# A modulation matrix loaded by channel chunks: the opening of a conformer and dilated-attention block on one Trainium2 core

## The chip, the cores and the metric

The kernel runs on one core of a Trainium2 chip. The metric is the device time of one execution in microseconds (us), as the median of several runs. Five engines run at once, each through its own instructions in a fixed order: TensorE (PE; its weight loads are listed as PEld), VectorE (DVE), ScalarE (ACT), GpSimd (POOL), and SyncE (SP), which here issues nearly all DMAs. An engine whose next instruction waits for a semaphore holds up everything behind it.

## The reference

One layer of a decoder block over 2048 tokens of 1024 channels, in float32. A conditioning vector `c` gives a shift and a scale per channel, the tokens are normalized and modulated, and one wide projection feeds a convolution branch and twelve attention heads:

```python
mod = silu(c) @ w_ada + b_ada                      # (1024) x (1024, 3072)
shift, scale, gate = jnp.split(mod, 3, axis=-1)
h = rms_norm(x, norm_w) * (1.0 + scale) + shift    # (2048, 1024)
z = h @ w_in                                       # a, b, g_conv, q, k, v, g_attn, m_conv, m_attn
q = rope(rms_norm(q, q_norm_w), positions); k = rope(rms_norm(k, k_norm_w), positions)
o = softmax-weighted sum of three dilated window attentions (4 heads each)
y = sigmoid(m_conv) * (conv branch @ w_conv_out) + sigmoid(m_attn) * (o * silu(g_attn) @ w_attn_out)
x = x + gate * (y @ w_out)
```

## The kernel before

Tokens go in 16 blocks of 128, channels in 8 chunks of 128. The modulated tokens `h` are kept transposed in SBUF for the whole projection, as two float32r parts `hT_hi` and `hT_lo`; each weight is split in the same way into `wh` and `wl`, and a projection is three matmuls per chunk (hi by wh, hi by wl, lo by wh), 24 for a block of tokens and 384 columns (`pz`, L305).

The program starts in this order. `c`, the biases and norm weights come in (`nat`, turned to `cols`); `sc` is silu of `c`. The rotary tables `tab` for all 16 blocks are made by DVE in operations over 1024 columns (L138 to L155), with two Sin on ACT. `w_ada`'s first 2048 columns come in 16 DMAs of whole rows (`wada`, L161), and PE multiplies `sc` with them in 64 matmuls (L163); the result is copied, turned into columns by 16 transposes (L171) and made into `mod` (L172, L173), which holds shift and scale for all channels. Only then can `h_first` make the first two token blocks of `h` (L223 to L230).

Then come the *units*: a unit is one attention head, with its 384 weight columns (q, k, v). Unit 0 has the extra work of making `h`: for a pair of token blocks, `x` is loaded (L190), squared and scaled on ACT (L199, L207) with the inverse root on POOL (L202, L106, L107), turned by PE (`pt_x`, L217, in four pieces of two chunks), and `h_part` makes `hf` (DVE, L238), `hT_hi` (ACT, L241) and `hT_lo` (DVE, L242). The piece for pair j+2 is turned inside the matmuls of blocks j and j+1. After its 24 matmuls each block has an end (`project_step`): squares on ACT (L322), inverse root on POOL, then on DVE norm weights (`qk`, L333), rotation (L340 to L343), and a store to `qkv_d` (L656). `t` banks of PSUM, two of them, take the turned pieces.

PE's order is that of the code, by hand. The other engines' orders are set by a list scheduler when the kernel is built, with its own estimates of durations; only instructions marked `keep_in_program_order` keep their place. A tile pool with `bufs=n` gives n buffers to a tag; a load into a buffer waits until all readers of the tile before it are done.

Of the kernel before, what the change touches and what calls it, by code (L numbers as in the profile page):

```python
# [10 lines left out]
F32 = mybir.dt.float32  # L11
# [7 lines left out]
P = 128  # L19
# [35 lines left out]
def tile_hybrid_block(  # L55
# [55 lines left out]

    tab = tabs.tile([P, NB, 2, 64], F32, tag="tab", name="tab0")
    with pool("start", side="right") as st:
        nat = st.tile([4 * KC, P], F32, name="nat")
        cols = st.tile([P, 4 * KC], F32, name="cols")
        nc.sync.dma_start(nat[:KC, :], c.rearrange("b (k p) -> (b k) p", p=P))
        nc.sync.dma_start(nat[KC : 3 * KC, :], b_ada[: 2 * D].rearrange("(k p) -> k p", p=P))
        nc.sync.dma_start(nat[3 * KC :, :], norm_w.rearrange("(k p) -> k p", p=P))
        nc.sync.dma_start(wqk[:, 0, :], q_norm_w[None, :].to_broadcast([P, P]))
        nc.sync.dma_start(wqk[:, 1, :], k_norm_w[None, :].to_broadcast([P, P]))  # L120
        pos_i = st.tile([P, NB], I32, name="pos_i")
        nc.sync.dma_start(pos_i, positions.rearrange("b (j p) -> p (b j)", p=P))
        freq = st.tile([P, 64], F32, name="freq")
        nc.sync.dma_start(freq, inv_freq[None, :].to_broadcast([P, 64]))

        pt = bank("t", "pt_c")
        nc.tensor.transpose(pt[:, : 4 * KC], nat, ident[: 4 * KC, : 4 * KC])
        nc.vector.tensor_copy(cols, pt[:, : 4 * KC])
        th = st.tile([P, KC], F32, name="th_c")
        nc.scalar.activation(th, cols[:, :KC], AF.Tanh, scale=0.5)  # L130
        nc.vector.scalar_tensor_tensor(sc, th, 1.0, cols[:, :KC], op0=ALU.add, op1=ALU.mult)
        nc.vector.tensor_scalar(sc, sc, 0.5, None, op0=ALU.mult)

        pos_f = st.tile([P, NB], F32, name="pos_f")
        nc.vector.tensor_copy(pos_f, pos_i)
        a = tab[:, :, 0, :]
        n = tab[:, :, 1, :]
        nc.vector.tensor_tensor(a, pos_f[:, :, None].to_broadcast([P, NB, 64]),  # L138
                                freq[:, None, :].to_broadcast([P, NB, 64]), op=ALU.mult)

        na = st.tile([P, NB, 64], F32, name="na")
        nc.vector.tensor_scalar(n, a, 1.0 / (2 * math.pi), MAGIC, op0=ALU.mult, op1=ALU.add)
        nc.vector.tensor_scalar(n, n, -MAGIC, None, op0=ALU.add)
        nc.vector.tensor_scalar(na, n, MAGIC * 2048, None, op0=ALU.add)
        nc.vector.tensor_scalar(na, na, -MAGIC * 2048, None, op0=ALU.add)
        nc.vector.tensor_sub(n, n, na)
        for part in TWO_PI:
            for t in (na, n):
                nc.vector.scalar_tensor_tensor(a, t, -part, a, op0=ALU.mult, op1=ALU.add)
        nc.vector.tensor_scalar(a, a, -PI_LO, PI_LO, op0=ALU.max, op1=ALU.min)  # L150
        nc.scalar.activation(n, a, AF.Sin)
        nc.scalar.activation(a, a, AF.Sin, scale=0.5)
        tc.keep_in_program_order(nc.scalar.activation(th[:, :1], th[:, :1], AF.Exp))
        nc.vector.tensor_tensor(a, a, a, op=ALU.mult)
        nc.vector.tensor_scalar(a, a, -2.0, 1.0, op0=ALU.mult, op1=ALU.add)  # L155

        acc = [bank("z", "ada0"), bank("z", "ada1"), bank("s", "ada2"), bank("s", "ada3")]
        for k in range(KC):
            for half in range(2):
                wa = st.tile([P, D], F32, tag="wa", name=f"wada{k}_{half}", bufs=10)  # L160
                last_ada = nc.sync.dma_start(wa, w_ada[P * k : P * k + P, D * half : D * half + D])  # L161
                for i in range(2):
                    nc.tensor.matmul(acc[2 * half + i][:1, :], sc[:, k : k + 1], wa[:, 512 * i : 512 * i + 512],  # L163
                                     start=(k == 0), stop=(k == KC - 1))
        row = st.tile([1, 2 * D], F32, name="row")

        for i in range(4):
            nc.scalar.activation(row[:, 512 * i : 512 * i + 512], acc[i][:1, :], AF.Copy)
        pa = bank("z", "pt_ada")
        for k in range(2 * KC):  # L170
            nc.tensor.transpose(pa[:, k : k + 1], row[:, P * k : P * k + P], ident[:1, :1])  # L171
        nc.vector.tensor_add(mod, pa[:, : 2 * KC], cols[:, KC : 3 * KC])  # L172
        nc.vector.scalar_tensor_tensor(mod[:, KC:], mod[:, KC:], 1.0, cols[:, 3 * KC :], op0=ALU.add, op1=ALU.mult)  # L173

# [12 lines left out]
    def load_x(j):  # L187

        xt = xp.tile([P, D], F32, tag="x", name=f"x{j}")
        i0 = nc.sync.dma_start(xt, x2[P * j : P * j + P, :])  # L190
        if j >= 4:
            tc.keep_in_program_order(i0)
# [27 lines left out]
    def h_first(kk, pt):  # L220
        for a in range(2):
            k = 2 * kk + a
            nc.scalar.activation(hi[:, k, :256], pt[:, 256 * a : 256 * a + 256], AF.Identity,  # L223
                                 scale=mod[:, KC + k : KC + k + 1], bias=mod[:, k : k + 1])
        for a in range(2):
            k = 2 * kk + a
            hf = xp.tile([P, 2, 256], F32, tag="hf", name=f"hf0_{k}", bufs=2)
            nc.vector.tensor_scalar(hf[:, 0], pt[:, 256 * a : 256 * a + 256], mod[:, KC + k : KC + k + 1],
                                    mod[:, k : k + 1], op0=ALU.mult, op1=ALU.add)
            (nc.gpsimd if a else nc.vector).tensor_tensor(lo[:, k, :256], hf[:, 0], hi[:, k, :256].bitcast(F32),  # L230
                                                          op=ALU.subtract)

# [11 lines left out]
    with tc.high_priority():  # L244
        for j in range(4):
            for f in load_x(j):
                f()
        turned = [h_turn(0, kk, "ttoo"[kk]) for kk in range(4)]

# [10 lines left out]
    def load_w(src, parts, tag, odd=None, pin=False, eng=nc.vector):  # L260
# [3 lines left out]
        def load(k):  # L264
            raw = wp.tile([P, 384], F32, tag="raw", name=f"raw_{tag}_{k}", bufs=3)
            off = 0
            for first, count, step in parts:
                w = P * count
                dst = raw[:, off : off + w].rearrange("p (s c) -> p s c", c=P)
                rowsk = src[P * k : P * k + P, :]  # L270
                if count == 1:
                    nc.sync.dma_start(raw[:, off : off + w], rowsk[:, first : first + P])
                else:
                    blk = rowsk.rearrange("p (s c) -> p s c", c=P)
                    b0, bs = first // P, step // P
                    nc.sync.dma_start(dst, blk[:, b0 : b0 + bs * (count - 1) + 1 : bs, :])
                off += w
# [20 lines left out]
    def z_tokens(pz, width, wh, wl, j, hooks, lo_last=False):  # L298
        terms = [(k, a, w[k]) for k in range(KC) for a, w in ((hi, wh), (hi, wl), (lo, wh))]
        if lo_last:  # L300
            terms.sort(key=lambda t: t[1] is lo)
# [220 lines left out]
    with tc.high_priority():  # L522
        for f in loads:
            f()
# [592 lines left out]
```

## Time and profile before

| | |
|---|---|
| median of 3 runs | 2532.13 us (2531.29 to 2532.79) |
| the profiled execution | 2532.06 us, of which the span is 2530.3 us |
| PE busy, of the span | 2495.4 us (99%) |
| DVE busy | 1663.2 us (66%) |
| ACT busy | 756.8 us (30%) |
| DMA, mean | 110 GB/s |

All times in the views are us from the span's start. A row of the timeline gives start, duration, engine, line, operation, output and inputs, shapes, how many, and in brackets how long the engine had been idle and for what it waited. "PEclk" is the granted clock of TensorE as a share of full speed.

### The profile page before, as it was taken

The page shows a single profiled execution, that of the slowest core. Times are in us where ns is not written, and L with a number is a line of the kernel's source. Part 1 is how long each engine was busy: PE and PEld are TensorE (multiplying, and loading weights), DVE is VectorE, ACT ScalarE, POOL GpSimd, SP SyncE. Part 2 cuts the span into 40 slices and gives each one's busy share as a digit, 9 for nine tenths or more (in the row PEclk, how much of TensorE's full clock was granted, in tenths as well). Part 3 has the DMA queues.
Part 4 walks back from the last instruction along what each step waited for, and adds up shares of the span by engine and source line. Part 5 has one row for each costly group of instructions (what it writes and reads, how often), then busy time and mean ns, then how long its engine had stood idle before and what let it go on. Part 6 is the DMA issues. An engine that isn't in the chain of part 4 may idle for free.

```text
span 2530.3 us, 38239 instructions
## 1 busy us (share of the span) xinstructions
PE 2495.4 (99%) x13377; PEld 2222.5 (88%) x13377; DVE 1663.2 (66%) x3522; ACT 756.8 (30%) x2366; POOL 250.1 (10%) x503
## 2 busy tenths in 40 slices
PE   7999999999999999999999999999999999999999
PEld 3989999999999999999888888888888878888887
DVE  5855655555555555566799999879697718774333
ACT  5733343344334434444111111111111114331010
POOL 3421111111111111122000000000000000000000
PEclk9999999999999999999999999999999999999999
DMA  6333533344321111144112122121212249867343
GB/s 228 116 106 113 160 111 97 100 118 122 108 75 55 56 36 40 52 130 149 41 47 70 64 80 83 39 70 60 63 65 68 99 147 328 296 211 230 124 134 111
DMA packets 262653, 278.51 MB, mean 110 GB/s; under 512 B 25464, under 2 KB 195736, under 8 KB 262462
## 3 DMA queue, kind: packets, MB, share of 16 engines
q1 hardware_dynamic: 262462, 276.07, 34.3%
q8 instruction: 106, 1.74, 0.3%
q14 instruction: 85, 0.70, 0.1%
HBM read 175.12 MB, written 100.86 MB: 109 GB/s over the span
## 4 chain that ended last, share of the span: by engine, by line
PE 95%; DMA 2%; ACT 1%; DVE 1%; POOL 1%; issue 0%; SPq 0%; POOLq 0%; DVEq 0%; ACTq 0%
PE pz L305 30%; PE pg L755 20%; PE yc L897 7%; PE out L897 7%; PE pb L755 7%; PE pa L755 7%; PE ya L897 3%; PE pzg L305 3%; PE ps L377 3%; PE po L396 3%; PE ptq L367 2%; PE ptp L388 1%; PE ada L163 1%; DMA fraw<-in_w_attn_out_dram 1%; DMA raw_u<-in_w_in_dram 0%
## 5 line engine op out<-in xcount | busy, mean ns | idle before, releaser
L784 DVE SCALAR_TENSOR_TENSOR ca<-up,chan,ca 128x1024 f32<-128x1024 f32 x480 | 593.2, 1280 | 3.7
L305 PE MATMUL pz<-wh_u,hT_lo 128*128 128x384 f32 x1536 | 536.2, 349 | 1.3 <-POOL hT_lo L230 0.7
L305 PE MATMUL pz<-wh_u,hT_hi 128*128 128x384 f32 x1536 | 516.9, 337 | 5.3 <-ACT wh_u L281 2.6
L305 PE MATMUL pz<-wl_u,hT_hi 128*128 128x384 f32 x1536 | 517.7, 337 | 0.6 <-DVE wl_u L284 0.4
L333 DVE SCALAR_TENSOR_TENSOR qk<-pz,st,wqk 128x128 f32<-128x128 f32 x384 | 116.9, 346 | 332.2 <-POOL st L107 332.1
L755 PE MATMUL pg<-hT_hi,wh_gm 128*128 128x512 f32 x768 | 298.7, 389 | 0.3 <-DVE gt L815 0.3
L755 PE MATMUL pg<-hT_lo,wh_gm 128*128 128x512 f32 x768 | 298.6, 389 | 0.0
L755 PE MATMUL pg<-hT_hi,wl_gm 128*128 128x512 f32 x768 | 297.9, 389 | 0.0
L305 PEld LDWEIGHTS pz<-wh_u,hT_hi 128*128 128x128 f32 x1536 | 289.7, 189 | 8.7 <-ACT wh_u L281 3.5
L305 PEld LDWEIGHTS pz<-wh_u,hT_lo 128*128 128x128 f32 x1536 | 289.2, 188 | 3.5 <-POOL hT_lo L230 1.3
L305 PEld LDWEIGHTS pz<-wl_u,hT_hi 128*128 128x128 f32 x1536 | 288.8, 188 | 1.8 <-DVE wl_u L284 1.4
L369 ACT ACTIVATE qkT<-ptq 128x256 f32<-128x256 f32 x192 | 74.0, 385 | 419.2 <-PE ptq L367 418.6
L813 ACT ACTIVATE gt<-pg 128x512 f32<-128x512 f32 x96 | 57.1, 597 | 422.2 <-PE pg L755 422.2
L755 PEld LDWEIGHTS pg<-hT_hi,wh_gm 128*128 128x128 f32 x768 | 144.1, 188 | 30.7 <-DVE gt L815 0.7
L755 PEld LDWEIGHTS pg<-hT_hi,wl_gm 128*128 128x128 f32 x768 | 144.2, 188 | 30.0
L755 PEld LDWEIGHTS pg<-hT_lo,wh_gm 128*128 128x128 f32 x768 | 144.1, 188 | 29.7
L107 POOL TENSOR_TENSOR st<-st,mhalf 128x2 f32<-128x2 f32 x192 | 136.7, 712 | 16.0
L322 ACT ACTIVATE sq<-pz 128x128 bf16<-128x128 f32 x384 | 106.2, 277 | 93.2 <-PE pz L305 86.4
L106 POOL TENSOR_SCALAR st<-st 128x2 f32<-128x2 f32 x192 | 45.7, 238 | 811.8 <-ACT sq L322 811.8
L382 ACT ACTIVATE sm<-sm,osb 128x128 f32<-128x128 f32 (+1 forms) x192 | 88.8, 462 | 64.4 <-DVE osb L380 61.3
L755 PE MATMUL pb<-hT_hi,wh_ab 128*128 128x512 f32 x256 | 99.7, 389 | 0.0
L755 PE MATMUL pa<-hT_hi,wh_ab 128*128 128x512 f32 x256 | 99.6, 389 | 0.0
(332 smaller groups left out, 4639.0 us busy)
## 6 DMA issues: line engine op xcount, KB each, us to landing
qkv_d<-qkv SPq DMA_DIRECT2D x128, 192.0 KB, 2.2
raw_u<-in_w_in_dram SPq DMA_DIRECT2D x96, 192.0 KB, 3.1
lqk<-qkv_d SPq DMA_DIRECT2D x128, 128.0 KB, 2.2
acc_d<-osb SPq DMA_DIRECT2D x192, 65.0 KB, 1.6
at<-acc_d SPq DMA_DIRECT2D x64, 195.0 KB, 3.3
x<-in_x_dram SPq DMA_DIRECT2D x16, 512.0 KB
wada<-in_w_ada_dram SPq DMA_DIRECT2D x16, 512.0 KB, 7.1
lv<-qkv_d SPq DMA_DIRECT2D x128, 64.0 KB, 1.8
```

The costliest lines, as they stand in the source:

```text
L107: nc.gpsimd.tensor_tensor(dst, scratch[:, :n], mhalf[:, :n], op=ALU.pow)
L305: nc.tensor.matmul(pz[:, :width], a[:, k, P * j : P * j + P], w[:, :width], start=(m == 0), stop=(m == 23))
L322: nc.scalar.activation(sq, pz[:, P * i : P * i + P], AF.Square, scale=1.0 / math.sqrt(P), accum_out=st[:, i : i + 1])
L333: nc.vector.scalar_tensor_tensor(qk[:, 2 * i : 2 * i + 2].rearrange("p a b -> p (a b)"), pz[:, P * i : P * i + P], st[:, 2 + i : 3 + i], w ...
L369: nc.scalar.activation(qkT.rearrange("p a b -> p (a b)"), pt[:, :256], AF.Copy)
L377: nc.tensor.matmul(ps[:, P * i : P * i + P], box["q"][:, 0, :], kt[:, 1, :], start=True, stop=True)
L382: nc.scalar.activation(sm[:, :w], sm[:, :w], AF.Exp, scale=-1.0, bias=o[:, P : P + 1], accum_out=o[:, P + 1 : P + 2])
L396: nc.tensor.matmul(po[:, :P], box["pT"][:, P * i : P * i + P], vt, start=(i == 0), stop=(i == nk - 1))
L755: nc.tensor.matmul(pz, w[k][:, P * col : P * col + P], a[:, k, 512 * t : 512 * t + 512], start=(m == 0), stop=(m == 23))
L784: nc.vector.scalar_tensor_tensor(accs[c], up[:, t0 + i : t0 + i + 1024], chan[:, cb, i : i + 1], accs[c], op0=ALU.mult, op1=ALU.add)
L813: nc.scalar.activation(th, pz, AF.Tanh, scale=0.5)
L897: nc.tensor.matmul(pz, w, xx, start=(m == 0), stop=(m == len(terms) - 1))
```

## The change

`w_ada` is no longer loaded by rows for all channels at once, but by chunk of 128 output channels: for chunk k two DMAs (`ada_load`), one for shift and one for scale, each of 128 partitions by 8 runs of 512 bytes. Tag `wa` has three buffers of 4 KB per partition in place of ten, so one and a half chunks. `ada_part` makes the 2 columns of `mod` for a chunk: of the eight pieces of each half, DVE sums five (multiplied by `sc`) into `sums`, and PE takes three and the sum, in matmuls of one column.

The first four token blocks are projected chunk by chunk: for each k, `h_make` makes 512 tokens of `hT_hi` and `hT_lo`, and twelve matmuls add this chunk to four open banks `pz0_0` to `pz0_3`; then comes `ada_part(k + 1)`, and the turn of x for chunk k + 2. The weights of unit 0 come in between, chunk by chunk. `x0` to `x3` are loaded from ACT's queue. The ends of these four blocks (`project_end`) and `h_part(4, ...)` follow after the loop.

The rotary tables are made in four pieces of four token blocks by `angles`, the first after the loop, the others beside blocks 4 and 8. Some attention tiles move to a pool `att`, opened at the end of unit 0; from the last blocks of unit 0 on the order of the engines is the one of before, but for a few places on DVE, ACT and SP in the last stages.

```diff
-    tab = tabs.tile([P, NB, 2, 64], F32, tag="tab", name="tab0")
-    with pool("start", side="right") as st:
...
-        for k in range(KC):
-            for half in range(2):
-                wa = st.tile([P, D], F32, tag="wa", name=f"wada{k}_{half}", bufs=10)
-                last_ada = nc.sync.dma_start(wa, w_ada[P * k : P * k + P, D * half : D * half + D])
-                for i in range(2):
-                    nc.tensor.matmul(acc[2 * half + i][:1, :], sc[:, k : k + 1], wa[:, 512 * i : 512 * i + 512],
-                                     start=(k == 0), stop=(k == KC - 1))
...
+    FIRST = 4
+    ON_DVE = 5
...
+    def ada_load(c0):
+        wa = [st.tile([P, KC, P], F32, tag="wa", name=f"wada{c0}_{half}", bufs=3) for half in range(2)]
+        for half in range(2):
+            c1 = D * half + P * c0
+            keep(nc.sync.dma_start(wa[half], w_ada[:, c1 : c1 + P].rearrange("(k p) c -> p k c", p=P)))
+        return wa
+
+    def ada_part(c0, wa):
+        pa = bank("o", f"pa{c0}")
+        for half in range(2):
+            sums = st.tile([P, P], F32, tag="sums", name=f"sums{c0}_{half}", bufs=2)
+            for k in range(ON_DVE):
+                if k == 0:
+                    nc.vector.tensor_scalar(sums, wa[half][:, 0], sc[:, :1], None, op0=ALU.mult)
+                else:
+                    nc.vector.scalar_tensor_tensor(sums, wa[half][:, k], sc[:, k : k + 1], sums,
+                                                   op0=ALU.mult, op1=ALU.add)
+            for k in range(ON_DVE, KC):
+                nc.tensor.matmul(pa[:, half : half + 1], wa[half][:, k], sc[:, k : k + 1],
+                                 start=(k == ON_DVE), stop=False)
+            nc.tensor.matmul(pa[:, half : half + 1], sums, ones[:, :1], start=False, stop=True)
+        both = mod[:, c0 : KC + c0 + 1 : KC]
+        nc.vector.tensor_add(both, pa[:, :2], cols[:, KC + c0 : 2 * KC + c0 + 1 : KC])
...
+    def h_make(k, pt):
+        scale, shift = mod[:, KC + k : KC + k + 1], mod[:, k : k + 1]
+        hs = hi[:, k, : P * FIRST]
+        nc.scalar.activation(hs, pt, AF.Identity, scale=scale, bias=shift)
+        hf = xp.tile([P, 512], F32, tag="hf", name=f"hf0_{k}", bufs=2)
+        nc.vector.tensor_scalar(hf, pt, scale, shift, op0=ALU.mult, op1=ALU.add)
+        nc.vector.tensor_tensor(lo[:, k, : P * FIRST], hf, hs.bitcast(F32), op=ALU.subtract)
...
+        for k in range(KC):
+            if k + 1 < KC:
+                loads[k + 1]()
+            if k + 2 < KC:
+                was[k + 2] = ada_load(k + 2)
+            h_make(k, turned.pop(k))
+            wh, wl = cur
+            for j in range(FIRST):
+                for i, (a, w) in enumerate(((hi, wh), (hi, wl), (lo, wh))):
+                    nc.tensor.matmul(pzs[j][:, :384], a[:, k, P * j : P * j + P], w[k],
+                                     start=(k == 0 and i == 0), stop=(k == KC - 1 and i == 2))
+            if k + 1 < KC:
+                ada_part(k + 1, was.pop(k + 1))
+            if k + 2 < KC:
+                turned[k + 2] = x_turn(k + 2)
...
+    angles(0, 4)
...
+                if u == 0 and j in (4, 8):
+                    angles(j + 4, 4)
```

How the built order moves shows in three places. First, SP's loads of `w_ada` (a name's digits are chunk and half). Before, ten buffers let the first ten go out with no wait for a reader:

```order
L161 DMA wada0_0_156<-in_w_ada_dram 128x1024 [waits DMAHW1_49]
L161 DMA wada0_1_160<-in_w_ada_dram 128x1024 [waits DMAHW2_49]
L161 DMA wada1_0_164<-in_w_ada_dram 128x1024 [waits DMAHW3_49]
L161 DMA wada1_1_168<-in_w_ada_dram 128x1024 [waits DMAHW4_49]
L161 DMA wada2_0_172<-in_w_ada_dram 128x1024 [waits DMAHW5_49]
```

Now, from the fourth on, each waits for the readers on DVE and PE of the tile three places ahead of it, so that `wada3_1` waits for those of `wada2_0`:

```order
L460 DMA wada2_1_244<-in_w_ada_dram 128x8x128 [waits DMAHW2_49,DVE_49,PE_49]
L192 DMA raw_u0_2_291<-in_w_in_dram 128x3x128 [waits DMAHW7_49]
L460 DMA wada3_0_297<-in_w_ada_dram 128x8x128 [waits DMAHW3_49,DVE_49,PE_49]
L460 DMA wada3_1_298<-in_w_ada_dram 128x8x128 [waits DMAHW1_49,DMAHW5_49,DVE_49,PE_49]
L192 DMA raw_u0_3_345<-in_w_in_dram 128x3x128 [waits Pool_49]
```

These loads moved from a queue of their own pace to one tied to the loop's use of them. Second, DVE at the start of `h`. Before, DVE had only `mod` and `h` there:

```order
L172 TENSOR_TENSOR mod_102<-pt_ada_225,cols_112 128x16 [waits PE_49]
L173 SCALAR_TENSOR_TENSOR mod_102<-mod_102,cols_112 128x8 [waits DVE_49]
L228 TENSOR_SCALAR hf0_0_375<-pt_x0_0_300,mod_102 128x256 [waits DVE_49,Activation_49]
L228 TENSOR_SCALAR hf0_1_378<-pt_x0_0_300,mod_102 128x256
L230 TENSOR_TENSOR hT_lo_249<-hf0_0_375,hT_hi_248 128x256 [waits DMAHW4_49,DMAHW3_49,DMAHW5_49,DMAHW2_49,DMAHW6_49,DMAHW1_49,DMAHW7_49,DMAHW0_49,DVE_49]
```

Now, in the loop's round for chunk 2, the first three operations on `wada3_1` stand ahead of `hf` and `hT_lo` of chunk 2:

```order
L478 TENSOR_TENSOR mod_102<-pa2_317,cols_128 128x2 [waits PE_49]
L480 SCALAR_TENSOR_TENSOR mod_102<-mod_102,cols_128 128x1 [waits DVE_49]
L469 TENSOR_SCALAR sums3_1_382<-wada3_1_298,sc_103 128x128 [waits DMAHW1_49]
L471 SCALAR_TENSOR_TENSOR sums3_1_382<-wada3_1_298,sc_103,sums3_1_382 128x128 [waits DVE_49] x2
L493 TENSOR_SCALAR hf0_2_356<-pt_x0_2_286,mod_102 128x512 [waits Activation_49]
L471 SCALAR_TENSOR_TENSOR sums3_1_382<-wada3_1_298,sc_103,sums3_1_382 128x128 [waits DVE_49]
L494 TENSOR_TENSOR hT_lo_112<-hf0_2_356,hT_hi_111 128x512 [waits DVE_49]
```

The sums of the next chunk moved into the making of this one. Third, ACT at block pair 12. Before, `x12`'s squares stood between the `hT_hi` of pairs 8 and 10:

```order
L199 ACTIVATE xn12_853,xst12_854<-x12_851 128x512 [waits DMAHW6_49]
L241 ACTIVATE hT_hi_248<-hf8_3_970 128x2x256 [waits DVE_49]
L199 ACTIVATE xn12_853,xst12_854<-x12_851 128x512 [waits Activation_49]
L241 ACTIVATE hT_hi_248<-hf10_0_1024 128x2x256 [waits DVE_49]
L207 ACTIVATE x12_851<-x12_851,xst12_854 128x512 [waits Pool_49]
```

Now they stand behind the last `hT_hi` of pair 10 and the Sin of the last table piece:

```order
L163 ACTIVATE hT_hi_111<-hf10_3_1278 128x2x256 [waits DVE_49]
L514 ACTIVATE tab0_107<-tab0_107 128x4x64 [waits DVE_49]
L515 ACTIVATE tab0_107<-tab0_107 128x4x64 [waits Activation_49]
L134 ACTIVATE xn12_995,xst12_996<-x12_993 128x512 [waits DMAHW6_49]
L134 ACTIVATE xn12_995,xst12_996<-x12_993 128x512 [waits Activation_49]
```

The normalization of `x12` moved behind a table piece that DVE makes beside block 8.

More of the change, by code (lines that the diff above doesn't have):

```diff
@@ L218, in h_turn @@
         return pt
[L220 to L231, printed above, removed]
     def h_part(j, kk):
@@ L258, in w_slots, with load_w @@
         return spare["pool"], "oh", "ol", 8
-    def load_w(src, parts, tag, odd=None, pin=False, eng=nc.vector):
+    def load_w(src, parts, tag, odd=None, pin=False, eng=nc.vector, early=False):
         wh, wl = [], []
```

168 lines of the change are left out of this document (93 added, 75 removed).

## The prediction

> **What bounds the kernel now.** I read the chain of waits first, then the busy times by stage, then the timelines of the opening. By chain and by stage:
>
> ```profile
> PE 95%; DMA 2%; ACT 1%; DVE 1%; POOL 1%; issue 0%; SPq 0%; POOLq 0%; DVEq 0%; ACTq 0%
> ```
> ```profile
> core 0: us, PE busy (x) PEld busy (x) DVE busy (x) ACT busy (x) POOL busy (x), PEclk, DMA share, GB/s
> 0.00:50.50 50.50, 34.83 (x97) 9.74 (x97) 21.30 (x23) 23.48 (x45) 17.14 (x31) 1.00 0.81 286
> 50.50:139.25 88.75, 84.78 (x505) 79.33 (x505) 75.95 (x189) 62.42 (x185) 36.91 (x70) 1.00 0.31 100
> ...
> 147.10:200.00 52.90, 52.88 (x316) 50.73 (x317) 27.06 (x97) 18.85 (x81) 9.86 (x22) 1.00 0.35 107
> ```
>
> The second row is unit 0, from its first matmul to its last; the third lies in unit 1. PE is nearly full there, but DVE is at 75.95 of 88.75 us too, 86%: it has little room. PE's timeline gives the corners:
>
> ```profile
> 19.02 29.34 PE L163 MATMUL ada<-wada,sc 128*1 128x512 f32 x64 [1.13 <-DVE tab L143]
> ...
> 50.51 0.44 PE L305 MATMUL pz<-wh_u,hT_hi 128*128 128x384 f32 x1 [1.06 <-ACT hT_hi L223]
> ...
> 138.90 0.34 PE L305 MATMUL pz<-wh_u,hT_lo 128*128 128x384 f32 x1
> 141.65 0.44 PE L305 MATMUL pz<-wh_u,hT_hi 128*128 128x384 f32 x1 [2.42 <-ACT wh_u L281]
> ...
> 143.05 0.52 PE L305 MATMUL pz<-wh_u,hT_hi 128*128 128x384 f32 x1
> 143.37 0.52 PE L305 MATMUL pz<-wl_u,hT_hi 128*128 128x384 f32 x1
> ```
>
> Nothing is projected before 50.51. Unit 0 ends at 139.24 us. From its last blocks on the order stays that of before, the stall at 139 to 147 included, so the change is worth what it moves this one point.
>
> **What it removes.** The 64 matmuls of 29.34 us leave PE, and with them the copies, the 16 turns and the empty PE up to 50.51. If all else fitted, up to some 30 us could go.
>
> **What it adds: a loop that waits for its own DMA.** In round k+1 the order on DVE is: three operations on the second half of chunk k+2, then `hf` and `hT_lo` of chunk k+1. PE's third matmul of the round needs that `hT_lo`; behind the twelve stands `ada_part(k + 2)`, and its three matmuls on the first half free the buffer into which the second half of chunk k+3 is loaded. DVE's next round begins with that load. So each round contains a whole load, issue to landing. The prices:
>
> ```profile
> 20.00:25.00 5.00, 5.00 (x10) 0.80 (x8) 4.86 (x6) 1.58 (x4) 2.25 (x3) 1.00 1.03 415
> 136.00:138.00 2.00, 2.00 (x13) 2.00 (x12) 1.63 (x6) 0.00 (x0) 0.00 (x0) 1.00 0.91 261
> ```
> ```profile
> DMA to landing us min/median/max: 2.7/3.8/6.2
> ```
>
> The windows show rate and DMA share. In the first, mostly `wada` rows of 4 KB, 415 GB/s; in the second, runs of 512 bytes (`raw_u`) and a store, 261 at a share of 0.91, so some 287 if full. The second fence is `raw_u`'s landing in units 0 to 2: 192 KB took 2.7 us at best. The new load has 512 KB in runs of 512 bytes: 2.7 plus 320 KB at 287 GB/s (1.1) is 3.8; I take 4.0, bounds 3.4 and 4.8. The Trainium skill (DMA: Bandwidth & Descriptors, Specifications) puts 512 bytes at line rate, which the two windows do not show; at its ceiling of 435 GB/s this load would be about 0.6 us shorter, an estimate, and the sum 4 us less over six rounds.
>
> DVE and PE in a round:
>
> ```profile
> 24.75 1.23 DVE L149 SCALAR_TENSOR_TENSOR tab<-na,tab 128x1024 f32<-128x1024 f32 x1
> 26.01 1.23 DVE L149 SCALAR_TENSOR_TENSOR tab<-tab 128x1024 f32<-128x1024 f32 x1
> ```
> ```profile
> L579 DVE SCALAR_TENSOR_TENSOR gate_sum<-wg,sc,gate_sum x14: 743/747/750, 246.3 to 315.9; 128x512 f32<-128x512 f32 x14
> ```
> ```profile
> L238 DVE TENSOR_SCALAR hf<-pt_x,mod 128x256 f32<-128x256 f32 x56 | 27.9, 538 | 5.3 <-PE pt_x L217 4.9
> L242 DVE TENSOR_TENSOR hT_lo<-hf,hT_hi 128x512 fp32r<-128x512 f32 x28 | 19.1, 684 | 0.7 <-ACT hT_hi L241 0.7
> L333 DVE SCALAR_TENSOR_TENSOR qk<-pz,st,wqk 128x128 f32<-128x128 f32 x30 | 9.1, 344 | 4.2 <-POOL st L107 4.2
> L340 DVE TENSOR_TENSOR t<-qk,tab 128x256 f32<-128x256 f32 x15 | 6.3, 418 | 0.1
> L342 DVE TENSOR_TENSOR qkv<-qkv,t 128x128 f32<-128x128 f32 x15 | 4.3, 284 | 0.1
> ```
> ```profile
> 60.36 0.44 PE pt_x L217 x4
> 147.12 15.53 PE pz L305 x88
> ```
>
> A sum step is L579's form over 128 columns: between 0.344 (L333) and 0.39 (L579 and L149 drawn on to 128), 0.03 more behind its predecessor (1.26 between the starts of two L149): 0.37. `hf` over 512 columns is 0.538 plus twice the 0.134 between L340 and L342, 0.81. A round: landing to `hT_lo` 0.25 + 2 x 0.37 + 0.81 + 0.15 (a sum step between) + 0.68 = 2.65; ten matmuls of 15.53 / 88 = 0.176 and three of at most 0.11 (L217's four in 0.44), 2.1; the end of the last, 0.2; the load, 4.0. Together 8.9 us.
>
> PE stands still for over 5 us of it. What that costs is shown behind the stall at 139 us:
>
> ```profile
> 139.50:140.00 0.50, 0.00 (x0) 0.00 (x0) 0.00 (x0) 0.00 (x0) 0.00 (x0) 1.00 0.15 35
> 142.50:143.00 0.50, 0.50 (x2) 0.50 (x3) 0.39 (x2) 0.50 (x4) 0.00 (x0) 0.50 0.00 0
> 145.50:145.75 0.25, 0.25 (x1) 0.07 (x1) 0.25 (x1) 0.00 (x0) 0.00 (x0) 1.00 0.72 211
> ```
>
> After 2.42 us without work the granted clock was 0.50 from 142 to 145.25, and matmuls started 0.32 us apart. A burst of a round is shorter than these 3.3 us, so I price all of it so: 3.2 + 0.6 in place of 2.1, 10.5 us a round; with full clock 8.9. The Trainium skill (TensorE: Matmul & The Clock Gate, HAM oscillation) tells of such a loop, small bursts between DMA waits of 3 to 5 us, each burst cold; the trace agrees in kind, with a shorter gap. By it the slow round is the rule.
>
> **The sum up to block 3.** The first x lands at 4.5 us; ACT then has eight squares and eight scales before the first `hT_hi`:
>
> ```profile
> 4.51 0.63 ACT L199 ACTIVATE xn<-x 128x512 bf16<-128x512 f32 x1 [2.51 <-DMA x<-in_x_dram]
> ```
> ```profile
> L207 ACT ACTIVATE x<-x,xst 128x512 f32<-128x512 f32 x32 | 21.5, 713 | 15.8 <-POOL xst L107 15.8
> L199 ACT ACTIVATE xn<-x 128x512 bf16<-128x512 f32 x32 | 20.1, 630 | 4.7 <-DMA x<-in_x_dram 4.4
> L199 ACT ACTIVATION_READ_ACCUMULATOR xn<-x 128x1 f32 x32 | 6.2, 195 | 0.0
> L241 ACT ACTIVATE hT_hi<-hf 128x512 fp32r<-128x512 f32 x28 | 17.5, 625 | 4.4 <-DVE hf L238 4.3
> ```
> ```profile
> 11.85 0.49 SPq L124 DMA_DIRECT2D freq<-in_inv_freq_dram  x1
> 15.30 1.43 DVE L138 TENSOR_TENSOR tab<-pos_f,freq 128x1024 f32<-128x1024 f32 x1 [1.66 <-DMA freq<-in_inv_freq_dram]
> ```
>
> 8 x 0.8 + 8 x 0.66 (pairs overlap a little) + two `wh` of 0.5 brings this to 17 us; `hT_hi`, `hf`, `hT_lo` and ten matmuls to 22.5, when the first half of chunk 1 is free. Six rounds of 10.5 bring it to 85.5. In the last round positions and `freq` (3.4 us from issue to use), queued behind the last loads on SP and ahead of `hf` on DVE, add 2.5; the rest of chunk 7 up to its `hT_lo` 3.5. That is 91.5.
>
> **From there to the end of unit 0.** Of the 75.95 us that DVE works in unit 0 now, three parts fall away behind the loop: `h_first` (12 operations, 5.2 us), one of the seven pairs of `h_part` (8 `hf` and 4 `hT_lo`, less their overlap, 6.1), and the three `wl` of unit 1 (1.5), which come late in both. That leaves 63.1 us. To it come the tables. They lay under the 50.5 us in which PE had other work; that cover is gone. In four pieces of 256 columns each operation pays its start again: some 4.6 us a piece for what is left, with eight steps near 0.4 to 0.46 and ten shorter ones, 18.5. Together 81.6. Kept at its present 86% this takes 95.3 us; without any wait, 81.6. I take 95, since two waits can be named: PE's third turn of pair 6 waits for an `hf` behind 12 us of block ends and table steps on DVE, and `x12`'s scaling stands on ACT behind a Sin whose input DVE makes late. PE's own work is shorter: 288 matmuls (51 us) and 96 turns (10.5).
>
> Unit 0 ends at 186.5 in place of 139.2: 47 us later. The profiled execution took 2532.06 us, the median is 2532.13. The forecast is 2579 us.
>
> The load of ACT's Exp table moves into unit 1, where ACT is busy for 18.85 of 52.9 us: nothing, or little over 1 us if that cover were gone. `x0` to `x3` leave SP's queue for ACT's at up to 0.5 us an issue (L124's row), before ACT has work.
>
> **Rivals.** (1) Clock full in the loop and DVE without waits behind it: rounds of 8.9 (10 us less) and 81.6 (13.7 less): 2555. For it: the gaps are short of what was seen only once. (2) The loads land early enough and the loop runs at DVE's pace: two halves of 1.75, `mod` 0.4, `hf` and `hT_lo` 1.4, 5.3 a round, 31 us less: 2548. Against it stands the waiting of `wada3_1` for PE. (3) Not slower: DVE's stream is never held. It has 0.5 + 28 (sums) + 3.2 (`mod`) + 10.8 (`h_make`) + 22 (tables) + 63.1 = 127.6 us; from 8.5 us on that ends at 136, 3 us ahead of before: 2529. It decides only while DVE is idle for less than 3 us in all; up to 8 us would still be within 0.2%. Against it: a load inside each round leaves DVE idle for some 4 us in each of six. (4) Both named tail waits at full length, some 13 us on PE before pair 12 alone, an estimate from the rows above (block ends and tables 6, Sin 1, squares and scales of two blocks 6): DVE then at 75% in place of 86%, 13 us more, 2592.
>
> **Chances.** Forecast 0.45; (1) 0.24; (2) 0.12; (3) 0.10; (4) 0.09. The range takes in (1), (2) and (4), and with the slowest load and ACT a little above: 2546 to 2600. 0.2% (5 us) is about what a measurement of this kernel tells from no change; slower 0.90; (3) is halved between the other two, faster by more, 0.06, since sum steps at L342's 0.284 would take another 7 us off, and within 0.04.
>
> **What would show it.** Right: in the loop a period near 10 us, DVE idle on `wada` loads some 4 us in each, granted clock below 1 from 25 to 85 us, and unit 0's last matmul near 186 us with the same distance to the end behind it. Wrong: loads that land within 2.5 us of issue, sum steps near 0.2 us, or a DVE over 95% busy from 10 us on.

## The result, and the profile after

The changed kernel takes 2599.07 us (median of 4 runs, 2598.59 to 2599.70) against 2532.46 us for the one before on the same chip: the ratio is 1.0263, with a 95% interval of 1.0246 to 1.0281. It is 66.6 us slower. The profiled execution has a span of 2596.8 us; before it was 2530.3.

The whole loss lies in the opening. The chain of waits shows the piece that stood at 147.12 us before:

```profile
213.71 15.54 PE pz L221 x88
```

213.71 less 147.12 is 66.59 us, and the spans differ by 66.5: from here on the two kernels take the same time. Unit 0's last matmul, at 138.90 us before, is now this one on PE's timeline, with a stall behind it as before:

```profile
206.63 0.34 PE L221 MATMUL pz<-wh_u,hT_lo 128*128 128x384 f32 x1
```

Busy times by stage: the loop, chunk 7 with the first work behind the loop, and the rest of unit 0 up to 1.2 us before its end:

```profile
core 0: us, PE busy (x) PEld busy (x) DVE busy (x) ACT busy (x) POOL busy (x), PEclk, DMA share, GB/s
20.00:91.90 71.90, 46.82 (x192) 42.01 (x192) 32.25 (x89) 7.80 (x12) 6.43 (x6) 0.60 0.39 106
91.90:104.10 12.20, 6.10 (x28) 5.50 (x28) 4.42 (x17) 10.29 (x24) 3.96 (x12) 0.64 0.52 185
104.10:205.80 101.70, 74.87 (x398) 70.98 (x399) 81.30 (x221) 54.36 (x161) 27.41 (x54) 0.82 0.24 80
```

In the loop nobody is full: PE is busy for 46.8 of 71.9 us, DVE for 32.3, the DMA engines are at a share of 0.39, and the mean granted clock is 0.60. One round, from the chain of waits:

```profile
47.13 3.69 DMA wada<-in_w_ada_dram
50.85 0.30 DVE sums L469
...
51.91 0.72 DVE hf L493
...
53.24 0.61 DVE hT_lo L494
53.90 3.57 PE pz L549 x10
57.47 1.08 PE pa L474 x6
58.57 3.76 DMA wada<-in_w_ada_dram
```

It is a closed circle: load, sums and `hT_lo`, ten matmuls (3.57 us, half speed), the small matmuls that free the buffer, the next load. DVE itself is idle on a load for only 1.2 to 2.0 us of such a round; it first sums the other half, and for that it waits longer, up to 4.9 us, until PE's matmul L476 is through. The first and the last of the six such loads, the last by its issue on SP:

```profile
24.90 4.00 DMA wada<-in_w_ada_dram
...
81.39 0.37 SPq L460
```

That is 56.5 us for five rounds, 11.3 each.

Behind the last load stands this on ACT:

```profile
84.03 0.78 ACT L491 ACTIVATE hT_hi<-pt_x,mod 128x512 fp32r<-128x512 f32 x1 [9.17 <-PE pt_x L485]
...
93.66 0.63 ACT L134 ACTIVATE xn<-x 128x512 bf16<-128x512 f32 x1 [6.67 <-DMA x<-in_x_dram]
...
101.72 0.76 ACT L491 ACTIVATE hT_hi<-pt_x,mod 128x512 fp32r<-128x512 f32 x1
```

`hT_hi` of chunk 7, the last row, comes 17.7 us after that of chunk 6: ACT first waits for the load of x4, then squares x4 to x7 and scales x4 and x5. And behind it PE's timeline has three long waits, ahead of the third turn of pair 6, in pair 8 and ahead of pair 12:

```profile
130.72 1.08 PE L152 MATMUL pt_x<-ident,x 128*128 128x128 f32 x4 [9.41 <-DVE hf L160]
...
141.61 0.69 PE L152 MATMUL pt_x<-ident,x 128*128 128x128 f32 x2 [3.59 <-ACT x L142]
...
173.98 0.47 PE L152 MATMUL pt_x<-ident,x 128*128 128x128 f32 x1 [9.27 <-ACT x L142]
```

### The profile page after: what moved, and what is told of

Its sections match the earlier page's. It is cut to its first block, busy times and chain, and to the rows that moved or that the text cites. A ratio compares the mean times of both kernels' runs of the same rounds, so it can differ in the third digit from the quotient of the medians.

```text
span 2596.8 us, 38483 instructions
## 1 busy us (share of the span) xinstructions
PE 2510.9 (97%) x13425; PEld 2257.8 (87%) x13425; DVE 1693.7 (65%) x3659; ACT 759.0 (29%) x2363; POOL 242.2 (9%) x499
## 3 DMA queue, kind: packets, MB, share of 16 engines
HBM read 175.12 MB, written 100.86 MB: 106 GB/s over the span
## 4 chain that ended last, share of the span: by engine, by line
PE 93%; DVE 2%; DMA 2%; ACT 1%; POOL 0%; issue 0%; SPq 0%; ACTq 0%; POOLq 0%; DVEq 0%
PE pz L221 29%; PE pg L805 20%; PE yc L947 7%; PE out L947 7%; PE pb L805 7%; PE pa L805 7%; PE ya L947 3%; PE pzg L221 3%; PE ps L296 3%; PE po L315 3%; PE ptq L286 2%; PE ptp L307 1%; DMA wada<-in_w_ada_dram 1%; PE pz L549 1%; ACT xn L134 0%
## 5 line engine op out<-in xcount | busy, mean ns | idle before, releaser
L221 PE MATMUL pz<-wh_u,hT_lo 128*128 128x384 f32 x1504 | 527.2, 351 | 0.8 <-DVE hT_lo L164 0.8
L221 PE MATMUL pz<-wh_u,hT_hi 128*128 128x384 f32 x1504 | 507.0, 337 | 3.0 <-ACT wh_u L199 2.5
L221 PE MATMUL pz<-wl_u,hT_hi 128*128 128x384 f32 x1504 | 508.1, 338 | 0.7 <-DVE wl_u L202 0.5
```

What stands on the lines that cost most here:

```text
L221: nc.tensor.matmul(pz[:, :width], a[:, k, P * j : P * j + P], w[:, :width], start=(m == 0), stop=(m == 23))
```

## The experiments

All are edits of the changed kernel. Times are medians of 4 runs, ratios are to the kernel before on the same chip. The experiments used four chips, on which the kernel before took 2530.6 to 2532.4 us, so a difference of one or two us between two rows can be the chip's. The last three columns come from the profiled execution: when `hT_hi` of chunk 7 starts on ACT (the end of the loop, but for one round's rest), the span, and the difference, which is what still follows.

| kernel | us | ratio (95%) | chunk 7 | span | rest |
|---|---|---|---|---|---|
| changed | 2599.07 | 1.0263 (1.0246 to 1.0281) | 101.72 | 2596.8 | 2495.1 |
| ring4 | 2591.55 | 1.0233 (1.0218 to 1.0249) | 94.78 | 2589.3 | 2494.5 |
| x45_early | 2607.76 | 1.0297 (1.0282 to 1.0312) | 109.71 | 2607.7 | 2498.0 |
| sums_on_pe | 2604.16 | 1.0294 (1.0263 to 1.0324) | 100.75 | 2594.3 | 2493.6 |
| pe_kept_busy | 2588.29 | 1.0226 (1.0211 to 1.0241) | 90.30 | 2586.5 | 2496.2 |
| x8_alone | 2599.50 | 1.0269 (1.0254 to 1.0285) | 101.36 | 2597.8 | 2496.4 |
| tables_in_loop | 2582.04 | 1.0198 (1.0182 to 1.0213) | 106.67 | 2580.1 | 2473.4 |
| tables_act | 2581.93 | 1.0205 (1.0188 to 1.0222) | 100.77 | 2579.0 | 2478.2 |
| two_rings | 2581.74 | 1.0201 (1.0186 to 1.0216) | 100.86 | 2579.1 | 2478.2 |
| two_rings_busy | 2581.22 | 1.0197 (1.0181 to 1.0212) | 99.05 | 2577.1 | 2478.1 |
| x8_ahead | 2571.74 | 1.0155 (1.0138 to 1.0172) | 100.70 | 2568.0 | 2467.3 |
| sums_first | 2557.68 | 1.0096 (1.0081 to 1.0111) | 84.56 | 2555.0 | 2470.4 |
| sums_split | 2554.64 | 1.0093 (1.0076 to 1.0110) | 76.06 | 2550.3 | 2474.2 |

### A fourth buffer for the weight: ring4

```diff
-        wa = [st.tile([P, KC, P], F32, tag="wa", name=f"wada{c0}_{half}", bufs=3) for half in range(2)]
+        wa = [st.tile([P, KC, P], F32, tag="wa", name=f"wada{c0}_{half}", bufs=4) for half in range(2)]
```

> The changed kernel with four buffers of 512 KB for the modulation weight in place of three, and nothing else. Theory (a whole load lies in each round, since the second half of a chunk can only be loaded when PE has freed a buffer that stands behind the twelve matmuls of the round before): with a fourth buffer the same load is issued almost a round earlier, the 4.0 us fall out of each of the six rounds, their period goes from 11.3 us to between 5.3 (DVE's own work) and 7.3, and the kernel is 24 to 36 us shorter: 2563 to 2575 us. Rival (the round is set by the chain DVE, PE and the half clock, and the load only lies beside it): period within 0.5 us of 11.3, 2595 to 2602 us.

Measured: 2591.55 us, 7.5 less, between theory and rival. The chain of waits from 44 us on has no load left in it, and is closed all the same:

```profile
44.13 0.44 PE pa L476 x2
44.59 0.30 DVE sums L469
...
48.75 0.70 DVE hT_lo L494
49.49 3.57 PE pz L549 x10
...
54.13 0.44 PE pa L476 x2
54.60 0.30 DVE sums L469
...
85.09 0.67 ACT hT_hi L491
```

The period is 10.0 us (44.59 to 54.60). DVE's first sum step waits for PE's matmul L476, which adds up the sums before: the tile `sums` has two buffers, one a half, and that matmul stands behind the twelve large ones. So the load was in the round, but it was the longer of two circles. The last row shows where more of the gain went: `hT_hi` of chunk 6 now stands on ACT behind the squares and scales of x4 and x5, much as chunk 7's does in the changed kernel, and came at 85.09 us, 18 us after chunk 5's.

### x4 and x5 earlier: x45_early

```diff
-        normed = {j: load_x(j, nc.scalar) for j in range(FIRST)}
+        normed = {j: load_x(j, nc.scalar) for j in range(FIRST + 2)}
...
             h_make(k, turned.pop(k))
+            if 1 <= k < 3:
+                for f in normed.pop(FIRST + k - 1):
+                    keep(f())
...
-        nc.scalar.activation(hs, pt, AF.Identity, scale=scale, bias=shift)
+        keep(nc.scalar.activation(hs, pt, AF.Identity, scale=scale, bias=shift))
```

> The changed kernel with x4 and x5 loaded behind x0 to x3 and normalised on ACT in the second and third round, and hT_hi of chunk 7 ahead of the squares of x6 and x7. Theory (the last round was lengthened by ACT, which stood at the squares of x4 to x7 until their loads had landed while hT_hi of chunk 7 was behind them): hT_hi of chunk 7 comes at about 90 us in place of 101.8, and what follows comes 8 to 12 us earlier: 2587 to 2591 us. Rival (behind the loop DVE is full whatever ACT does, with the first table piece and four block ends waiting): 0 to 3 us, 2596 to 2599 us.

Measured: 2607.76 us, 8.7 more. The edit moved other things than it meant to. The first weight load, which took 8.26 us from its issue in the changed kernel, shares the DMA engines with two more x; and `freq`, whose load is now what the first table step waits for, stands ahead of `hf` of chunk 6 on DVE:

```profile
1.90 10.93 DMA wada<-in_w_ada_dram
...
91.78 6.23 DMA freq<-in_inv_freq_dram
```

With every `hT_hi` pinned the scheduler also put all sum steps of a half ahead of `hf`, and rounds took some 12.5 us. The run says nothing on ACT's order; tables_act asks again.

### No sums on DVE: sums_on_pe

```diff
-    ON_DVE = 5
+    ON_DVE = 0
...
-            nc.tensor.matmul(pa[:, half : half + 1], sums, ones[:, :1], start=False, stop=True)
```

> The changed kernel with all eight partial products of a modulation half as matmuls of one column on PE; the five sum steps a half on DVE and the matmul that adds them up are left out (the result is the same sum). Theory (the load is in the round because DVE's sums of the second half stand ahead of hf and hT_lo): with the sums on PE behind the twelve matmuls, a load has the whole of hf, hT_lo and the twelve matmuls to land in, some 5 us; the round is then 16 small matmuls of 0.17 us at half clock (2.7), mod 0.4, hf and hT_lo 1.7, the matmuls 3.6: 8.4 us, 2.9 less in each of six rounds, 17 us: 2582 us, and down to 2570 where the clock rises. Rival (DVE's 28 us of sums are themselves what the opening lacks): 28 us less, 2571 us, with rounds of 5 to 6 us. Third possibility, that PE's stream gets longer by as much: 2599 us.

Measured: 2604.16 us; its runs spread from 2596.1 to 2612.5, so no more can be said than that nothing was gained. In its profile DVE works only some 15 us between 25 and 100, where it worked 35, and a round still takes 10.2 us (55.35 to 65.55). No load is in it:

```profile
55.35 3.57 PE pz L541 x10
58.92 3.76 PE pa L467 x32
...
63.15 0.79 ACT hT_hi L483
...
64.81 0.70 DVE hT_lo L486
65.55 0.69 PE pz L541
```

DVE's 28 us of sums were not what the loop lacked: without them the rival had rounds of 5 to 6 us. The sixteen small matmuls took 3.76 us in place of the expected 2.7: each goes in two passes (x32), which the expectation had counted as one. With `mod`, `hT_hi`, `hf` and `hT_lo` in sequence behind them they fill the room of the load.

### The tables inside the loop: tables_in_loop

```diff
         was = {0: ada_load(0)}
+        keep(nc.scalar.dma_start(pos_i, positions.rearrange("b (j p) -> p (b j)", p=P)))
+        keep(nc.scalar.dma_start(freq, inv_freq[None, :].to_broadcast([P, 64])))
...
+            if k == 2:
+                nc.vector.tensor_copy(pos_f, pos_i)
+            if 2 <= k < 6:
+                angles(4 * (k - 2), 4)
...
-    keep(nc.sync.dma_start(pos_i, positions.rearrange("b (j p) -> p (b j)", p=P)))
-    keep(nc.sync.dma_start(freq, inv_freq[None, :].to_broadcast([P, 64])))
...
-    nc.vector.tensor_copy(pos_f, pos_i)
-    angles(0, 4)
...
-    angles(4, 4)
...
-                if u == 0 and j in (4, 8):
-                    angles(j + 4, 4)
```

> The changed kernel with positions and frequencies loaded at the start on ACT's queue and the four table pieces made in rounds 2 to 5 of the loop, where DVE waits for the load, in place of behind it. Theory (the 18.5 us of the tables cost their full length in the tail, since DVE is what the tail waits for, and cost nothing in the loop, where DVE has about 4 us idle in each round): unit 0 ends 18 to 21 us earlier, 2.5 us of it from the queue of the last round: 2578 to 2581 us. Rival (each round gets longer by a piece, since the sums stand behind it): 2595 to 2600 us. Second rival (the tail waits for ACT and PE, not for DVE): less than 8 us, 2591 us or more.

Measured: 2582.04 us, 17.0 less, 1 us short of the theory. The loop ended 5 us later, although positions and `freq` no longer hold up its last round, and what follows it became 21.7 us shorter (2495.1 to 2473.4 in the table). Behind the loop the pieces cost more than the 18.5 us that the prediction gave them, since waits hang on them: those ahead of the third turn of pair 6 and ahead of pair 12 are gone here. Inside the loop they were cheap, but not free.

### ACT's order in the last round: tables_act

```diff
+        if k == KC - 1:
+            keep(ins)
...
     for j in range(FIRST, FIRST + 2):
         for f in normed.pop(j):
-            f()
+            keep(f())
```

> The kernel of tables_in_loop, and on ACT hT_hi of chunk 7 kept ahead of the squares and scales of x4 to x7; the loop's order up to there stays as it was. Theory (ACT's order costs what the loads of x4 to x7 last: in tables_in_loop x4 landed at 97.35 us and hT_hi of chunk 7 ran at 106.77, behind five squares, scales and their statistics): hT_hi of chunk 7 at 97 to 98 us, unit 0 ends 8 to 10 us earlier: 2572 to 2575 us. Rival (x4 and x5 are what PE needs next anyway, so the order only changes who is late): less than 3 us, 2579 to 2583 us.

Measured: 2581.93 us against 2582.04, the rival's figure, though `hT_hi` of chunk 7 did run 5.9 us earlier (100.77 for 106.67). SP's timeline shows what was late instead:

```profile
111.24 14.26 SPq L572 DMA_DIRECT2D qkv_d<-qkv  x4
125.58 1.42 SPq L127 DMA_DIRECT2D x<-in_x_dram  x3
```

The loads of x8 to x10 stand on SP's queue behind the stores of blocks 0 to 3, and the fourth store waits for DVE's last step on block 3.

### Both circles opened: two_rings

```diff
-            sums = st.tile([P, P], F32, tag="sums", name=f"sums{c0}_{half}", bufs=2)
+            sums = st.tile([P, P], F32, tag="sums", name=f"sums{c0}_{half}", bufs=4)
```

with ring4's edit, on the kernel of tables_act.

> The kernel of tables_act with four buffers for the modulation weight and four for the sums. Theory (the loop is closed twice: by the weight's three buffers through a load, and by the two sums buffers through PE, since DVE's first sum step of chunk k+2 waits for the matmul that adds up chunk k+1, which stands behind the twelve matmuls at half clock; in ring4 the first was gone and the period was still 10.0 us): with both gone DVE's work sets the period, 5.3 us and 9.9 where a table piece is in it, or PE's at half clock, 7.7; from 11.8 us in tables_in_loop this is 4 x 1.9 + 2 x 4.1 = 16 us less: 2556 to 2560 us. Rival (DVE and PE hold each other through hT_hi, hf and hT_lo whatever buffers there are): a period above 10.5 us, 2568 us or more.

Measured: 2581.74 us, no change from the 2581.93 of tables_act. The chain of waits has the load back:

```profile
42.10 5.42 DMA wada<-in_w_ada_dram
47.54 0.29 DVE sums L469
47.83 0.61 DVE hT_lo L496
48.48 3.57 PE pz L553 x10
52.05 1.07 PE pa L474 x6
...
54.86 5.49 DMA wada<-in_w_ada_dram
```

With four `sums` buffers free, the scheduler that sets DVE's order put a sum step on a chunk two further on, whose load is not yet there, ahead of `hT_lo`. The added room was spent on looking further ahead, and the circle closed again, at 12.8 us.

### PE kept at work: pe_kept_busy and two_rings_busy

```diff
+    def warm(c0):
+        for i in range(14):
+            nc.tensor.transpose(pas[c0][:, 128:256], ident, ident)
...
             if k + 2 < KC:
                 turned[k + 2] = x_turn(k + 2)
+            if k + 1 < KC:
+                warm(k + 1)
```

> The changed kernel with fourteen turns of a constant added on PE behind each round's turns, into columns of the bank pa that nobody reads; nothing else. Theory (the half clock costs what the matmul rows say, since PE stands still for over 4 us in a round): if the added work keeps the granted clock at 1.00, the twelve matmuls of a round take 2.1 us in place of 3.9 and the small ones and the turns 1.3 us less; of that 2 to 3 us lie on the round's path: 12 to 18 us less, 2581 to 2587 us, with matmuls 0.176 us apart. Rival (the clock stays at half, and the added 14 x 0.22 us only push the next matmuls): 2598 to 2606 us.

> The kernel of two_rings with six such turns a round. Theory: with the matmuls at full clock PE's round is some 4.5 us, so DVE alone sets it; two_rings less 4 to 10 us: 2548 to 2556 us. Rival (DVE already sets the round of two_rings): within 2 us of two_rings.

Measured: 2588.29 us for the first, 10.8 less than the changed kernel and 1.3 outside the theory's range. The clock was granted more of the time (0.60 in the same window of the changed kernel), and PE's timeline shows it rise among the large matmuls behind the added turns:

```profile
25.00:75.00 50.00, 40.37 (x251) 38.73 (x251) 28.42 (x77) 6.60 (x11) 7.12 (x5) 0.83 0.47 128
```
```profile
51.61 0.52 PE L555 MATMUL pz<-wl_u,hT_hi 128*128 128x384 f32 x1
51.93 0.43 PE L555 MATMUL pz<-wh_u,hT_lo 128*128 128x384 f32 x1
...
52.37 0.34 PE L555 MATMUL pz<-wl_u,hT_hi 128*128 128x384 f32 x1
52.55 0.35 PE L555 MATMUL pz<-wh_u,hT_lo 128*128 128x384 f32 x1
```

Matmuls go from 0.32 us apart to 0.18. From there two rounds took 8.2 and 8.4 us (`hT_hi` at 48.17, 56.39 and 64.77), against 11.3: some 3 us are the price of the half clock in a round. It did not last: from 69 us on the large matmuls were 0.32 us apart again, and that round took 10.1 us. (The scheduler also put `hT_hi` of chunk 7 ahead of some squares here, so the 10.8 us are not all the clock's.) In two_rings_busy six turns a round were added and the time, 2581.22 us, stayed: its loop ended only 1.8 us earlier.

### SP's queue: x8_ahead and x8_alone

```diff
-    normed = {j: load_x(j) for j in range(FIRST, FIRST + 4)}
+    normed = {j: load_x(j) for j in range(FIRST, FIRST + 6)}
...
-    normed = {j: load_x(j) for j in range(FIRST + 4, FIRST + 6)}
```

> The kernel of tables_act, with the loads of x8 and x9 issued on SP behind those of x4 to x7 and so ahead of the stores of blocks 0 to 3. Theory (tables_in_loop, tables_act and two_rings all came to 2582 us with loops that ended 6 us apart, because x8 and x9 stand on SP's queue behind the store of block 3, which waits for the last block end on DVE: in tables_act they were issued at 125.58 us and PE's turns of pair 8 began at 135.97): x8 lands by 105 us, the wait ahead of pair 8 goes, and unit 0 ends 8 to 14 us earlier: 2568 to 2574 us. Rival (DVE and ACT need that time for blocks 0 to 7 anyhow): less than 3 us, 2579 to 2583 us.

> The changed kernel with the loads of x8 and x9 issued on SP ahead of the stores of blocks 0 to 3; the order on ACT, DVE and PE stays as it was. Theory (in the changed kernel, too, the wait ahead of pair 8 is SP's queue: x8 to x10 were issued at 127.95 us, behind the stores): PE's turns of pair 8 begin some 8 us earlier than 141.61 us, 2589 to 2593 us. Rival (there the squares of x8 stand on ACT behind the Sin of the table piece for blocks 8 to 11, whose input DVE finishes at 133.2 us, so the load is not what is late; that is why taking the tables away gave 17 us): less than 2 us, 2597 to 2600 us.

On the kernel of tables_act this gave 2571.74 us, 10.2 less, as the theory had it. On the changed kernel itself it gave nothing (2599.50 us), as its rival had it. ACT's timeline shows why, the first fence of the changed kernel, the second of x8_alone, where x8 was issued nearly 40 us earlier:

```profile
133.19 0.42 ACT L514 ACTIVATE tab<-tab 128x256 f32<-128x256 f32 x1 [0.17 <-DVE tab L513]
...
133.96 0.61 ACT L134 ACTIVATE xn<-x 128x512 bf16<-128x512 f32 x1
```
```profile
132.82 0.42 ACT L514 ACTIVATE tab<-tab 128x256 f32<-128x256 f32 x1 [0.17 <-DVE tab L513]
...
133.60 0.61 ACT L134 ACTIVATE xn<-x 128x512 bf16<-128x512 f32 x1
```

The square of x8 stands on ACT behind a Sin whose input DVE has just made, and so comes when DVE is through with that table piece. Two locks hold the same door, pair 8: SP's queue and, through ACT, the tables on DVE. Opening the queue alone gave nothing. Taking the tables away alone gave its 17.0 us at other doors, pairs 6 and 12, while PE's wait at pair 8 grew from 3.59 to 4.27 us (5.12 in tables_act), with SP's queue now behind it. With both gone that wait is gone too, and the kernel is 10.2 us shorter.

### PE's order turned round: sums_first and sums_split

```diff
+        h_make(0, turned.pop(0))
         for k in range(KC):
...
-            h_make(k, turned.pop(k))
+            if k + 1 < KC:
+                ada_part(k + 1, was.pop(k + 1))
+                h_make(k + 1, turned.pop(k + 1))
...
             wh, wl = cur
             for j in range(FIRST):
...
-            if k + 1 < KC:
-                ada_part(k + 1, was.pop(k + 1))
```

`sums_first` puts the sums and `hT` of the next chunk ahead of this chunk's matmuls, on the kernel of x8_ahead, with four weight buffers and `ON_DVE = 0`, and loads x4 to x9 in the last rounds. `sums_split` sets `ON_DVE = 4`, makes two table pieces before the loop and scales x1 and x3 on DVE.

> The kernel of x8_ahead with four buffers for the modulation weight, all sums on PE (as in sums_on_pe), the sums and hT of chunk k+1 ahead of the twelve matmuls of chunk k in every engine's order, and x4 to x9 loaded in the last three rounds. Theory (each serial step of the round that the runs named is gone: the load, the sums on DVE, the wait of hT for the matmuls of the chunk before): a round is PE's own work, 16 small matmuls, twelve large ones and four turns, 4.4 us at full and 7.5 at half clock, beside 1.2 MB of loads (4.2 us at 287 GB/s); from 23 us on eight rounds end between 58 and 83 us, and DVE's 63.1 us at 86 per cent bring unit 0 to 131 to 156 us against 139.24 before: 2524 to 2549 us. Rival (behind the loop x, ACT and the queue decide whatever the loop takes): unit 0 ends later than 165 us, 2558 us or more.

> The kernel of sums_first with four sum steps a half on DVE again and four as matmuls, two table pieces made before the loop and two in it, and x1 and x3 scaled on DVE. Theory (in sums_first PE was busy without a gap from 23.4 to 75 us, 9.5 us a chunk, and the sixteen small matmuls took 3.6 to 6.6 us of it): ten small ones instead, 2 to 3 us less a round, the loop ends some 16 to 22 us earlier, and unit 0 at 138 to 145 us: 2531 to 2541 us, level with before at best. Rival (DVE, with its sums back, is late by as much, as in the changed kernel): 2550 to 2560 us.

Measured: 2557.68 and 2554.64 us, the first at the edge of its rival (2558 or more), the second within its rival. The loop ended at 84.56 and 76.06 us. In sums_first PE had no gap from 23 to 75 us, but a chunk cost 8.4 us of it, and one 11.5, since the large matmuls ran at half clock (last section). In sums_split the loop ended 8.5 us earlier, and about half of that was given back behind it, where the rest grew from 2470.4 to 2474.2; by their ratios the two kernels are not told apart. Neither beats the kernel before: with a rest of 2467 to 2474 us, its span of 2530.3 asks for chunk 7 at 56 to 63 us.

## Why the prediction was right, and where it was short

The forecast was 2579 us, range 2546 to 2600, slower. The time is 2599.07: on the forecast side, with a mechanism that the trace confirms, but 20.1 us above the forecast and only 0.9 below the end of the range. No errors cancel here: each of the four terms came out longer than it was put. By the prediction's own steps, the end of unit 0 is at 207.0 in place of 186.5, 20.5 us late; the stall behind it, which was to stay as it was, is 1.1 us shorter than before (6.74 us for 7.88).

- **Start, 22.5 us: 24.9.** 2.4 short.
- **A whole load in each round: right.** Every round of the chain has one, of 3.7 to 4.1 us for a term of 4.0. A round's length was 11.3 and not 10.5 us (the terms as given add up to 10.6), 4.0 over the five rounds between the first and the last of the six loads. The terms that were small, in the round shown: landing to `hT_lo` 3.0 for 2.65 (50.82 to 53.85), the ten matmuls 3.57 for 3.2, and the freeing matmuls 1.08 for 0.6, since each of the three goes in two passes. That the load decides alone was too simple: ring4 found a second circle 1.3 us shorter behind it.
- **Half clock: right.** 0.60 in the loop. By the Trainium skill (TensorE: Matmul & The Clock Gate, HAM oscillation) such bursts between waits run cold each time; the trace agrees, with the ten matmuls of each round in the loop 0.32 us apart. The reason given, that a burst is shorter than the 3.3 us seen at half clock, does not hold, since the ten matmuls alone took 3.57 us. With PE kept at work the clock was 0.83 and its full-clock rounds 8.3 us, where the prediction had 8.9.
- **The last round, 16.5 us with 2.5 for the queue and 3.5 for chunk 7: 22.7 us** (81.39 to 104.1). This term failed by 6.2. From the load's issue to the start of `hT_lo` it took 11.1 us (81.39 to 92.46) where the round before took 6.4 (69.62 to 75.99), so positions, `freq` and what DVE does with them ahead of `hf` cost some 4.7 and not 2.5. And it did not count that x4 to x7's squares stand on ACT ahead of `hT_hi` of chunk 7: DVE had `mod` of chunk 7 ready at 98.7 us, and `hT_hi` came at 101.72. tables_act turned that order and got chunk 7 5.9 us earlier, in a kernel where this alone brought no time.
- **The tail, 95 us: 102.9** (104.1 to 207.0). DVE's work was sized well, 81.3 us against 81.6; its share was not, 79% for 86%. Both named waits came, 9.41 us ahead of pair 6's third turn and 9.27 ahead of pair 12, somewhat shorter than rival (4) had them (about 12 and 13 us); the forecast had kept them inside the share of before. Rival (4) gave the tail 108 us, so the measured one lies between the two. That the tables are what holds the tail, tables_in_loop showed with 17.0 us. The loads of x8 behind SP's stores were not named; in the changed kernel itself they cost nothing (x8_alone).

Of the rivals, (1) is refuted by the clock and DVE's 79%, (2) by the loads in the chain: even with a fourth buffer the round was 10.0 and not 5.3 us. (3) needed DVE idle for less than 3 us in all; in the loop alone it is idle for some 40 of 71.9 us. By the time alone (4), 2592, came nearer than the forecast, but more than half of what was missing lies ahead of the tail, where (4) changed nothing. Of the signs asked for, the period (11.3 us for near 10) and the clock came. Unit 0's end came late. And DVE was idle on `wada` loads for 1.2 to 2.0 us a round and not for 4: most of its waiting was for PE's L476, the second circle, which could thus be seen before ring4 opened the first.

The table gives the sum a second way: in the six kernels with the tables behind the loop the rest is 2493.6 to 2498.0 us, so each microsecond of the loop passed through to the time.

What stays open: how much of the last round's 6.2 us ACT's order costs in the changed kernel itself, where no run turned it without other moves in the schedule. By the trace it is at most the 3.0 us from 98.7 to 101.72.

## What to carry to other kernels

Where a change puts a load inside a loop, draw every circle: which instruction frees the buffer, what stands ahead of it on its engine, and what that waits for; opening the longest circle gains only the distance to the next, which an engine's other waits in the same round give away (here DVE's 4.9 us for L476), and a list scheduler may spend an added buffer on looking ahead and close the circle again. Split a trace at one fixed instruction (here the last `hT_hi` of the loop) and compare the two sides between kernels: the side that did not move tells whether a gain was lost or only not made. Before work is moved out of a cover into a stretch at 86%, name every queue behind it, SP's and ACT's as well: a lock can show nothing while a second one holds the same door, as SP's queue, worth nothing in the changed kernel, was worth 10.2 us once the tables were gone.

## What the runs showed of the hardware

In sums_first PE's records leave no gap, and yet the clock fell. Windows over sixteen matmuls of one column, over the twelve large ones behind them, and over the next sixteen:

```profile
34.50:38.40 3.90, 3.90 (x34) 3.90 (x32) 0.00 (x0) 0.52 (x1) 1.00 (x1) 0.87 0.24 65
38.40:42.50 4.10, 4.10 (x14) 4.00 (x14) 1.82 (x4) 0.78 (x1) 0.00 (x0) 0.50 0.84 241
43.40:50.00 6.60, 6.60 (x32) 6.60 (x33) 0.00 (x0) 0.46 (x1) 1.00 (x1) 0.50 0.27 79
```

I had expected gaps alone to bring it down. In this loop the large matmuls of seven rounds, each behind sixteen small ones, all began 0.32 us apart, the spacing of half clock. The small ones were not slow throughout: in five rounds the sixteen took 3.6 to 4.5 us, in two 6.7, of which the last row is one. So the clock rose and fell again within rounds in which PE was never idle; what in them brings it down, no run here separates. In the changed kernel the gaps were also short, with two matmuls between them (PE's timeline):

```profile
38.53 0.69 PE L549 MATMUL pz<-wh_u,hT_hi 128*128 128x384 f32 x1 [1.68 <-ACT hT_hi L491]
...
42.47 0.69 PE L549 MATMUL pz<-wh_u,hT_lo 128*128 128x384 f32 x1 [2.93 <-DVE hT_lo L494]
```

The granted clock in the windows can also read too high. In x45_early it is 1.00 from 20 to 52 us, while the large matmuls of these rounds start 0.32 us apart:

```profile
20.00:52.00 32.00, 22.00 (x78) 19.40 (x77) 14.46 (x34) 8.50 (x18) 6.14 (x9) 1.00 0.30 83
```
```profile
24.42 0.52 PE L552 MATMUL pz<-wl_u,hT_hi 128*128 128x384 f32 x1
24.74 0.52 PE L552 MATMUL pz<-wh_u,hT_lo 128*128 128x384 f32 x1
```

So in an opening the spacing of the matmuls decides, not the clock column.
